# Regrouping the end of a state-space scan: weight sums by DMA, lag matrices later, two units split like the others

## The chip, the cores and the metric

The kernel runs on one core of one Trainium2 chip. The metric is the device time of one execution in microseconds. The engines are PE (matrix products), DVE (vector), ACT (scalar), POOL (GpSimd) and SP, which here only issues DMAs. ACT and POOL issue DMAs too. Each engine works through its own queue in order.

## The reference

One layer of a diffusion backbone over 1024 latent tokens with 256 context tokens, width 1024. The mixer is a two-directional diagonal state-space model; a SwiGLU block and a final norm follow.

```python
def s5_direction(u_ctx, u_lat, lam_re, lam_im, log_step, b_re, b_im, c_re, c_im):
    ...
    def run(u, h0):
        bu = jnp.einsum('lgh,gnh->lgn', u.astype(F32), b_bar)
        bu = bu.at[0].add(lam_bar * h0)
        a = jnp.broadcast_to(lam_bar, bu.shape)
        _, h = lax.associative_scan(_linear_combine, (a, bu), axis=0)
        return jnp.einsum('lgn,ghn->lgh', h, c_mat).real, h[-1]
    y_c, h_c = run(u_ctx, jnp.zeros(lam_bar.shape, lam_bar.dtype))
    y_l, _ = run(u_lat, h_c)
...
    def out(y, h):
        y = y.reshape(h.shape).astype(h.dtype) + d_skip * h
        g = jax.nn.gelu(y)
        return g * jax.nn.sigmoid(g @ w_glu + b_glu)
...
x = x + m_l[2][:, None] * y_l
h_l = modulate(rms_norm(x, norm_ffn[i]), m_l[3][:, None], m_l[4][:, None])
x = x + m_l[5][:, None] * swiglu(h_l, ffn_w1[i], ffn_w3[i], ffn_w2[i])
...
return rms_norm(x, norm_final)
```

There are 64 groups of 16 channels, each with 64 complex states per direction. Everything is float32.

## The kernel before, in words

**Tiling.** Tokens are cut into blocks of T = 8. Block states are scanned over 160 columns (32 of context, 128 of latent tokens), and inside a block the output is a Toeplitz product. The 64 groups form 4 quarters of 16, and each quarter two units of 8 groups: units 0 and 1 are quarter 0, units 6 and 7 quarter 3. A unit's mixer output is therefore the sum of a Toeplitz product of its inputs (`x_mm`, line 945, full height of 128 blocks) and of the products of the scanned states with the output weights `CL` (`states_mm`, line 922, one half of the 128 blocks; `states_all`, line 935, both halves). The backward direction needs its states in turned order: `turned` copies them.

**Scan.** `scan()` runs on DVE (line 77): 32 steps of two columns, then 63 of one. Each step has two products and two adds over all quarters. In its first, two-column part, the columns in between are left out; they are restored by quarter: quarters 0 and 2 by DVE in the gaps of the scan, quarters 1 and 3 by POOL, with `fill`, each call of which restores half the columns for all 16 elements.

**Work beside the scan.** `PROG1` is an order written out by hand for PE, ACT, POOL and SP, which run beside DVE's scan; `PROG2` is the order after it. Each token is a letter with an index:

- A: products of the modulation weights (line 531). B: turned input weights. M, m: modulation rows and columns.
- L, G: load of a quarter's output coefficients and sign change of part of them.
- C qp: part p (0 to 3) of quarter q of the output weights `CL`: two products on POOL, 128 x 1024 each, and their sum. `HOWS` says how the sum is made: E, an add on POOL (line 677); P, by PE through the identity, with two copies on ACT (lines 672, 673); Y, an accumulating DMA issued by POOL (line 675). `cts` names the temporary of the second product.
- F: restores left out columns on POOL.
- K: half of a quarter's lag matrices (`k_mats`, lines 809 to 817), copied out by ACT and written to DRAM from its queue (lines 821, 822). K needs all four parts of its quarter's `CL`.
- T u: loads a piece of a Toeplitz matrix from there (line 830, SP's queue), two pieces to a unit, into four places that are used in turn.
- R k: turned early half of unit k (on ACT). P k: Toeplitz and early states of unit k on PE, in two PSUM tiles. Y: copies of these to SBUF (line 993, ACT).
- After the scan: Z k, turned late half, on the engine that `ZEN` names (line 904 or 902); N k, late states of unit k; D k, their add to the early part on DVE; H k, GELU on ACT; I and J, transposes and their split for the GLU; W, V, w, l, x, g: GLU weights, gates and products.

In the kernel before, units 0 to 5 go this way: early part in `PROG1`, late states after the scan. Units 6 and 7 are left whole until after the scan: z copies all 128 turned columns, Q makes the Toeplitz product and all states at once, and GELU reads the two PSUM tiles.

**PSUM.** Tiles tagged `w` (`pw`) have three places that are used in turn: a new tile waits until the last reader of the tile in its place is through. K takes two accumulators, `kt` and `pm`; K6 takes two zeroed `pw` tiles.

Of the kernel before, what the change touches and what calls it, by code (L numbers as in the profile page):

```python
# [13 lines left out]
AF = mybir.ActivationFunctionType  # L14
# [3 lines left out]
P = 128  # L18
# [17 lines left out]
LN2H = 0.693359375
LN2L = -2.12194440e-4
# [5 lines left out]
def s5_ffn_kernel(tc, a, out):  # L43
# [3 lines left out]
    with ctx:  # L47
# [611 lines left out]
        def cl_ops(q, part, ct, how):  # L659
# [7 lines left out]
            def add():  # L667
# [8 lines left out]
                else:  # L676
# [232 lines left out]
        def yview(k, gp):  # L909
            return Y[:, k].rearrange("p t (a e h) -> p e a t h", e=2, h=HC)[:, gp]  # L910

        def states_mm(k, pts, half, hs, start):

            for a_ in range(4):
                for ri in range(2):
                    for d in range(2):
                        cs_ = slice(64 * (half ^ d), 64 * (half ^ d) + 64)
                        c0 = 31 + 64 * half
                        for gp in range(2):
                            ps = slice(64 * gp, 64 * gp + 64)  # L920
                            st = hs[ps, :, ri, a_] if d else STQ[k // 2][ps, c0:c0 + 64, ri, 8 * (k % 2) + a_]
                            PE.matmul(flat(pts[gp][cs_, a_]), st, flat(CL[k // 2][ps, ri, d, 4 * (k % 2) + a_]),
                                      start=start and ri == 0, stop=ri == 1 and (start or a_ == 3))

        def states_all(k, pts, hs):

            for a_ in range(4):
                for ri in range(2):
                    for d in range(2):
                        for c in range(2):  # L930
                            cs_ = slice(64 * c, 64 * c + 64)
                            for gp in range(2):
                                ps = slice(64 * gp, 64 * gp + 64)
                                st = hs[ps, cs_, ri, a_] if d else STQ[k // 2][ps, 31 + 64 * c:95 + 64 * c, ri, 8 * (k % 2) + a_]
                                PE.matmul(flat(pts[gp][cs_, a_]), st, flat(CL[k // 2][ps, ri, d, 4 * (k % 2) + a_]),
                                          start=False, stop=a_ + ri + d == 5)

        def x_mm(k, pool):

            pts = [pool([4, T, HC]) for _ in range(2)]  # L940
            for a_ in range(4):
                for gp in range(2):
                    g = 2 * a_ + gp
                    kq = KQ[(2 * k + g // 4) % 4][:, g % 4].rearrange("p (t h) -> p t h", t=T)[:, ::-1]
                    PE.matmul(pts[gp][:, a_], U[:, 8 * k + g, 32:160], kq, start=a_ == 0, stop=False)
# [3 lines left out]
        inner = {}
        HSe = [view(r, kb, [64, 2, 4]) for r, kb in ((RC[3], 14), (RC[3], 12), (RC[3], 14), (RC[3], 12), (RA, 2), (RA, 0))]  # L950
        HSl = [view(RA, STB * (i // 3) + 4.125 + 2 * (i % 3), [64, 2, 4]) for i in range(6)]
        HSq = {6: view(RA, 0, [P, 2, 4]), 7: view(RA, STB, [P, 2, 4])}

        def run(prog):


            for w in prog.split():
                op, i = w[0], int(w[1:])
                if op == "A":
                    ada(i)  # L960
                elif op == "M":
                    mod_cols(i)
                elif op == "K":
                    k_mats(*divmod(i, 2), [zeros(pw([15 * HC])) if i == 6 else kt, zeros(pw([15 * HC])) if i in (0, 1, 2, 3, 6) else pm[:, 0:15 * HC]])
                elif op == "L":
                    cs_load(i, S)
                elif op == "G":
# [4 lines left out]
                elif op == "C":  # L972
                    q, part = divmod(i, 10)
                    for f in cl_ops(q, part, cts[q][part], HOW[q][part]):
                        f()
                elif op == "F":
                    fill(*divmod(i, 10), *((RW, 0) if i >= 30 else (RC[3], 12)))
                elif op == "T":
                    toeplitz(i)
                elif op == "R":  # L980
                    turned(i, 0, HSe[i], S)
                elif op == "Z":
                    turned(i, 1, HSl[i], ENG[ZEN[i]])
                elif op == "z":
                    turned(i, 2, HSq[i], ENG[ZEN[i]])
                elif op == "P":
                    inner[i] = x_mm(i, pw)
                    states_mm(i, inner[i], 0, HSe[i], False)
                elif op == "Q":
                    inner[i] = x_mm(i, pe8)  # L990
                    states_all(i, inner[i], HSq[i])
                elif op == "Y":
                    S.copy(yview(i // 2, i % 2), inner[i // 2][i % 2])
# [774 lines left out]
```

## Time and profile before

| what | us |
|---|---|
| median of 3 runs (lowest, highest) | 1016.93 (1014.88, 1017.97) |
| profiled execution, its own time | 1015.21 |
| its span, first to last instruction | 1013.4 |
| PE busy | 959.4 |
| DVE busy | 780.4 |
| POOL busy | 763.4 |
| ACT busy | 438.9 |

The span is what the profile's rows add up to; the time of an execution is 1.8 us more. Busy times are sums over stages with different limits. The stage of the change lies between 129 us (the scan's first step) and about 260 us (the first GLU products). In the rows, `x4` behind an instruction is a count, a bracket holds the idle time before it and what ended that, and windows give busy times with counts, then the granted PE clock, the share of the DMA engines and GB/s.

### The profile page before, as it was taken

Reading aid. Unit: us, or ns where it says so; the run is one execution under the profiler, and the core shown is the slowest. Engines: PE = TensorE matmul, PEld = TensorE weight load, DVE = VectorE, ACT = ScalarE, POOL = GpSimd, SP = SyncE. Lnnn points to the kernel's source line nnn. Section 1 sums busy time; section 2 is a strip of 40 time slices with the busy share of each in tenths; the row PEclk is TensorE's granted clock in tenths of the full one; section 3 lists DMA queues with packets and bytes.
Section 4 is the critical chain, followed back from the end, with each engine's and each line's share of the span. In section 5 each row is a group of like instructions: output and inputs, shape, how many; then the busy total and the mean of one; then the engine's idle time right before and its main releaser. Section 6 shows DMA issues by size and latency. Waiting matters only on the chain. (4 is left out here: it accounts for less than half of the span.)

```text
span 1013.4 us, 18560 instructions
## 1 busy us (share of the span) xinstructions
PE 959.4 (95%) x6988; PEld 772.1 (76%) x6988; DVE 780.4 (77%) x1638; ACT 438.9 (43%) x860; POOL 763.4 (75%) x590
## 2 busy tenths in 40 slices
PE   5988798779999999999999999999999999999996
PEld 1466523679999988778888888888888888888885
DVE  7989699996356867877958677686959677686987
ACT  5478622335444663443343343324343343324337
POOL 5799998994672448979785878777786878777764
PEclk9999999999999999999999999999999999999998
DMA  9765997334512021011212111121212111121205
GB/s 336 280 135 95 280 346 247 95 84 138 188 46 80 2 104 63 27 44 46 73 42 83 42 52 42 50 66 53 73 42 83 43 52 43 46 70 53 73 22 166
DMA packets 48546, 98.96 MB, mean 98 GB/s; under 512 B 4284, under 2 KB 18876, under 8 KB 47176
## 3 DMA queue, kind: packets, MB, share of 16 engines
q1 hardware_dynamic: 43272, 86.64, 26.0%
q0 software_dynamic: 2016, 7.34, 3.9%
q10 hardware_dynamic: 3168, 3.79, 1.1%
q8 instruction: 55, 0.90, 0.4%
q14 instruction: 35, 0.29, 0.1%
HBM read 84.25 MB, written 6.17 MB: 89 GB/s over the span
## 5 line engine op out<-in xcount | busy, mean ns | idle before, releaser
L77 POOL TENSOR_TENSOR c<-rxc,c 128x512 fp32r<-128x512 f32 x128 | 166.6, 1315 | 53.5 <-ACT c L1222 52.7
L1282 PE MATMUL ut<-ra,c 128*128 128x512 f32 x400 | 155.7, 389 | 1.2 <-DVE ra L77 1.2
L1281 PE MATMUL ut<-ra,c 128*128 128x512 f32 x400 | 155.7, 389 | 0.2 <-ACT ra L1222 0.2
L1283 PE MATMUL ut<-ra,c 128*128 128x512 f32 x400 | 155.6, 389 | 0.0
L1222 ACT CAST c<-rxc 128x512 fp32r<-128x512 f32 x128 | 79.1, 622 | 147.0 <-PE xt L1576 53.3
L1576 PE MATMUL xt<-c,c 128*128 128x512 f32 x540 | 129.7, 389 | 0.0
L1576 PEld LDWEIGHTS xt<-c,c 128*128 128x128 f32 x540 | 101.4, 188 | 21.0
L77 DVE TENSOR_TENSOR ru<-ru,xt 128x1024 f32<-128x1024 f32 x90 | 107.3, 1215 | 10.9 <-PE xt L1576 7.9
L77 DVE TENSOR_TENSOR ru<-ut,ru 128x512 f32<-128x512 f32 x98 | 67.2, 686 | 43.0 <-PE ut L1283 37.6
L1282 PEld LDWEIGHTS ut<-ra,c 128*128 128x128 f32 x400 | 75.1, 188 | 17.0 <-POOL rxc L77 1.5
L1281 PEld LDWEIGHTS ut<-ra,c 128*128 128x128 f32 x400 | 75.1, 188 | 16.1 <-ACT ra L1222 0.6
L1283 PEld LDWEIGHTS ut<-ra,c 128*128 128x128 f32 x400 | 75.1, 188 | 15.5
L77 POOL TENSOR_TENSOR c<-rw,c 128x512 fp32r<-128x512 f32 (+1 forms) x29 | 41.1, 1417 | 37.8 <-ACT c L1222 37.8
L77 POOL TENSOR_TENSOR c<-ru,c 128x512 fp32r<-128x512 f32 (+1 forms) x39 | 57.1, 1465 | 10.1 <-ACT c L1222 5.7
L1281 PE MATMUL ut<-c,c 128*128 128x512 f32 x160 | 62.3, 390 | 0.8 <-DVE rxa L77 0.8
L77 POOL TENSOR_TENSOR rxc<-rxc 128x512 f32<-128x512 f32 x40 | 61.4, 1535 | 1.6
L1282 PE MATMUL ut<-c,c 128*128 128x512 f32 x160 | 62.2, 389 | 0.0
L1283 PE MATMUL ut<-c,c 128*128 128x512 f32 x160 | 62.2, 389 | 0.0
L1576 PE MATMUL ut<-c,c 128*128 128x512 f32 x216 | 51.9, 389 | 0.0
L584 PE MATMUL pv<-ru,c 128*64 128x160 f32 x512 | 45.0, 316 | 5.6 <-ACT rxa L388 1.8
L77 DVE TENSOR_TENSOR pe<-pe,ru 128x256 f32<-128x256 f32 x64 | 27.4, 429 | 29.5 <-ACT pe L1122 17.4
L77 DVE TENSOR_TENSOR ru<-ru,ut 128x512 f32<-128x512 f32 x76 | 47.3, 680 | 0.3
(444 smaller groups left out, 2569.1 us busy)
## 6 DMA issues: line engine op xcount, KB each, us to landing
c<-in_ada_w SPq DMA_DIRECT2D x46, 256.0 KB
rxc<-in_w SPq DMA_DIRECT2D x38, 256.0 KB
rxc<-in_w SPq DMA_DIRECT2D x19, 512.0 KB
ru<-in_w SPq DMA_DIRECT2D x11, 512.0 KB
rw<-in_w SPq DMA_DIRECT2D x11, 512.0 KB
ra<-in_ada_w SPq DMA_DIRECT2D x10, 512.0 KB
ra<-in_ada_w SPq DMA_DIRECT2D x18, 256.0 KB
ru<-in_xT SPq DMA_DIRECT2D x4, 1024.0 KB
```

What stands on the lines that cost most here:

```text
L77: eng.tensor_tensor(out=o, in0=x, in1=y, op=op)
L584: PE.matmul(pv[64 * (i % 2):64 * (i % 2) + 64, ri, c0:c0 + 160], w[:, i, 64 * ri:64 * ri + 64], U[:, 8 * b + 4 * j + i], start=True, stop= ...
L1222: S.copy(o[0], x)
L1281: PE.matmul(pu, wh, bh, start=start, stop=False)
L1282: PE.matmul(pu, wh, bl, start=False, stop=False)
L1283: PE.matmul(pu, wl, bh, start=False, stop=stop)
L1576: PE.matmul(pd, w[:, cs_], b, start=j in (1, 2, 4) and n == 0, stop=n == 2, skip_group_check=j not in (1, 2, 4))
```

## The change

- Five of the weight sums that POOL made are now accumulating DMAs (C21, C22, C30, C31, C32); the sum of C33 goes to PE. C23 stays on POOL. Before, C21 to C23 and C30 to C33 were all adds on POOL. A fifth temporary is added, in columns of quarter 1 that units 2 and 3 read early.
- Quarter 3 is restored by unit: `fill_k`, 8 elements at a time over all left out columns, in four POOL operations of 512 columns in place of eight of 256. F6 and F7 replace F30 and F31.
- Units 6 and 7 get early halves in `PROG1` (R6 P6 Y12 Y13, R7 P7 Y14 Y15), states only; unit 7's go to a scratch place. Their Toeplitz products come after the scan, in N6 and N7, in the same PSUM tiles as the late states; D6 and D7 add the parts. `states_all`, z and Q are gone.
- K4 goes behind P2 and next to K5, which gets two zeroed `pw` tiles (O5); O6 does the same ahead of K7 and K6, behind C33.
- Units 4 and 5: states first, then the Toeplitz product, in the same tiles.
- C33 goes from ahead of R5 to behind Y11.

```diff
-HOWS = "PPPP PPEE PEEE EEEE"
+HOWS = "PPPP PPEE PYYE YYYP"
-PROG1 = ("... T6 T7 C21 C22 C23 K4 R2 P2 Y4 Y5 K5 R3 P3 Y6 Y7 T8 T9 T10 T11 C30 C31 R4 P4 Y8 Y9 C32 C33 R5 P5 Y10 Y11 K7 K6 M2 m0 F30 F31")
-PROG2 = ("T12 T13 T14 T15 Z0 N0 Z1 Z2 D0 Z3 N1 D1 Z4 H0 H1 N2 D2 H2 w0 w1 l1 N3 Z5 D3 H3 N4 D4 z6 z7 I0 J0 I1 J1 H4 N5 D5 I2 J2 H5 I3 J3 W0 W1 x0 x1 x2 x3"
-         " Q6 H6 I4 J4 Q7 b0 I5 J5 H7 g03 g13 I6 J6 g23 g05 g15 I7 J7 V1 w20 w21 g26 x10 x11 x12 x13")
+PROG1 = ("... T6 T7 C21 C22 C23 R2 P2 Y4 Y5 O5 K4 K5 R3 P3 Y6 Y7 T8 T9 T10 T11 C30 C31 R4 P4 Y8 Y9 C32 R5 P5 Y10 Y11 C33 O6 K7 K6 M2 m0 F6 R6 P6 Y12 Y13 F7 R7 P7 Y14 Y15")
+PROG2 = ("T12 T13 T14 T15 Z0 N0 Z1 Z2 D0 Z3 N1 D1 Z4 H0 H1 N2 D2 H2 w0 w1 l1 Z6 N3 Z5 D3 H3 Z7 N4 D4 I0 J0 I1 J1 H4 N5 D5 I2 J2 H5 I3 J3 W0 W1 x0 x1 x2 x3"
+         " N6 D6 H6 I4 J4 N7 D7 b0 I5 J5 H7 g03 g13 I6 J6 g23 g05 g15 I7 J7 V1 w20 w21 g26 x10 x11 x12 x13")
...
-        cts = [..., [ct_[1], ct_[2], ct_[0], ct_[1]], [ct_[3], ct_[0]] * 2]
+        ct_ = [..., (RA, STB + 4.125)]
+        cts = [..., [ct_[1], ct_[3], ct_[0], ct_[2]], [ct_[3], ct_[0], ct_[4], ct_[3]]]
...
+        def fill_k(k):
+            tmps = [view(RA, 4.25 + 2 * i, [512]) for i in range(2)]
+            st, e = STQ[k // 2], 8 * (k % 2)
+            rot(st[:, 32:95:2, :, e:e + 8], st[:, 31:94:2, :, e:e + 8], LS[:, 0], 8 * k, E, tmps)
...
+        def ypart(k, gp):
+            return view(RA, 2 * STB + 4.25 + 2 * gp, [4, T, HC]) if k == 7 else yview(k, gp)
...
         def x_mm(k, pool):
-            pts = [pool([4, T, HC]) for _ in range(2)]
+            new = not isinstance(pool, list)
+            pts = [pool([4, T, HC]) for _ in range(2)] if new else pool
...
+                elif op == "O":
+                    KO[i] = [zeros(pw([15 * HC])) for _ in range(2)]
...
                 elif op == "P":
-                    inner[i] = x_mm(i, pw)
-                    states_mm(i, inner[i], 0, HSe[i], False)
+                    inner[i] = x_mm(i, pw) if i < 4 else [pw([4, T, HC]) for _ in range(2)]
+                    states_mm(i, inner[i], 0, HSe[i], i >= 4, i not in (4, 5))
+                    if i in (4, 5):
+                        x_mm(i, inner[i])
...
                 elif op == "N":
-                    late[i] = [pe8([4, T, HC]) for _ in range(2)]
-                    states_mm(i, late[i], 1, HSl[i], True)
+                    late[i] = [pe8([4, T, HC]) for _ in range(2)] if i < 6 else x_mm(i, pe8)
+                    states_mm(i, late[i], 1, HSl[i], i < 6)
                 elif op == "D":
-                        tt(yview(i, gp), po, yview(i, gp), ADD)
+                        tt(yview(i, gp), po, ypart(i, gp), ADD)
                 elif op == "H":
-                    if i in late:
-                        S.activation(Y[:, i], Y[:, i], AF.Gelu_apprx_tanh)
-                    else:
-                        for gp in range(2):
-                            S.activation(yview(i, gp), inner[i][gp], AF.Gelu_apprx_tanh)
+                    S.activation(Y[:, i], Y[:, i], AF.Gelu_apprx_tanh)
```

More of the change, by code (lines that the diff above doesn't have):

```diff
@@ L29 @@
 MAGIC = 12582912.0
-HOWS = "PPPP PPEE PEEE EEEE"
+HOWS = "PPPP PPEE PYYE YYYP"
 ZEN = "VVSVSVSV"
-PROG1 = ("A22 B0 A26 C02 G1 A30 A34 C03 A40 K0 A44 A48 C10 K1 L2 A54 G2 C11 A60 F10 C12 F11 C13 T0 T1 T2 T3 A64 M0 M1 K2 R0 P0 Y0 Y1 K3 L3 R1 C20 P1 Y2 Y3 T4 T5 G3 T6 T7 C21 C22 C23 K4 R2 P2 Y4 Y5 K5 R3 P3 Y6 Y7 T8 T9 T10 T11 C30 C31 R4 P4 Y8 Y9 C32 C33 R5 P5 Y10 Y11 K7 K6 M2 m0 F30 F31")
-PROG2 = ("T12 T13 T14 T15 Z0 N0 Z1 Z2 D0 Z3 N1 D1 Z4 H0 H1 N2 D2 H2 w0 w1 l1 N3 Z5 D3 H3 N4 D4 z6 z7 I0 J0 I1 J1 H4 N5 D5 I2 J2 H5 I3 J3 W0 W1 x0 x1 x2 x3"
-         " Q6 H6 I4 J4 Q7 b0 I5 J5 H7 g03 g13 I6 J6 g23 g05 g15 I7 J7 V1 w20 w21 g26 x10 x11 x12 x13")
+PROG1 = ("A22 B0 A26 C02 G1 A30 A34 C03 A40 K0 A44 A48 C10 K1 L2 A54 G2 C11 A60 F10 C12 F11 C13 T0 T1 T2 T3 A64 M0 M1 K2 R0 P0 Y0 Y1 K3 L3 R1 C20 P1 Y2 Y3 T4 T5 G3 T6 T7 C21 C22 C23 R2 P2 Y4 Y5 O5 K4 K5 R3 P3 Y6 Y7 T8 T9 T10 T11 C30 C31 R4 P4 Y8 Y9 C32 R5 P5 Y10 Y11 C33 O6 K7 K6 M2 m0 F6 R6 P6 Y12 Y13 F7 R7 P7 Y14 Y15")
+PROG2 = ("T12 T13 T14 T15 Z0 N0 Z1 Z2 D0 Z3 N1 D1 Z4 H0 H1 N2 D2 H2 w0 w1 l1 Z6 N3 Z5 D3 H3 Z7 N4 D4 I0 J0 I1 J1 H4 N5 D5 I2 J2 H5 I3 J3 W0 W1 x0 x1 x2 x3"
+         " N6 D6 H6 I4 J4 N7 D7 b0 I5 J5 H7 g03 g13 I6 J6 g23 g05 g15 I7 J7 V1 w20 w21 g26 x10 x11 x12 x13")
 LOG2E = 1.4426950408889634
@@ L693, in s5_ffn_kernel @@
                  14: [(3, range(4), 0, 8)]}
-        ct_ = [view(r, kb, [8, T, HC]) for r, kb in ((RW, 0), (RC[3], 0), (RC[3], 4), (RA, STB))]
-        cts = [[ct_[0], ct_[0], ct_[1], ct_[2]], [ct_[0], ct_[1], ct_[2], ct_[0]], [ct_[1], ct_[2], ct_[0], ct_[1]], [ct_[3], ct_[0]] * 2]
+        ct_ = [view(r, kb, [8, T, HC]) for r, kb in ((RW, 0), (RC[3], 0), (RC[3], 4), (RA, STB), (RA, STB + 4.125))]
+        cts = [[ct_[0], ct_[0], ct_[1], ct_[2]], [ct_[0], ct_[1], ct_[2], ct_[0]], [ct_[1], ct_[3], ct_[0], ct_[2]], [ct_[3], ct_[0], ct_[4], ct_[3]]]
         CL0 = cl_ops(0, 0, cts[0][0], SY) + cl_ops(0, 1, cts[0][1], SY)
@@ L864, in scan, with fill_q @@
                 one()
-        def fill(q, h, reg, kb):
-            tmps = [view(reg, kb + i, [256]) for i in range(2)]
+        def fill_q(q, h):
+            tmps = [view(RC[3], 12 + i, [256]) for i in range(2)]
             st, c0 = STQ[q], 32 * h
@@ L910, in yview, with states_mm @@
             return Y[:, k].rearrange("p t (a e h) -> p e a t h", e=2, h=HC)[:, gp]
-        def states_mm(k, pts, half, hs, start):
+        def ypart(k, gp):
+            return view(RA, 2 * STB + 4.25 + 2 * gp, [4, T, HC]) if k == 7 else yview(k, gp)
+        def states_mm(k, pts, half, hs, start, stop=True):
             for a_ in range(4):
@@ L922, in states_mm @@
                             PE.matmul(flat(pts[gp][cs_, a_]), st, flat(CL[k // 2][ps, ri, d, 4 * (k % 2) + a_]),
[L923 to L931, printed above, removed]
-                            for gp in range(2):
[L933 to L936, printed above, removed]
+                                      start=start and a_ + ri == 0, stop=stop and ri == 1 and a_ == 3)
         def x_mm(k, pool):
-            pts = [pool([4, T, HC]) for _ in range(2)]
+            new = not isinstance(pool, list)
+            pts = [pool([4, T, HC]) for _ in range(2)] if new else pool
             for a_ in range(4):
@@ L944, in x_mm @@
                     kq = KQ[(2 * k + g // 4) % 4][:, g % 4].rearrange("p (t h) -> p t h", t=T)[:, ::-1]
-                    PE.matmul(pts[gp][:, a_], U[:, 8 * k + g, 32:160], kq, start=a_ == 0, stop=False)
+                    PE.matmul(pts[gp][:, a_], U[:, 8 * k + g, 32:160], kq, start=new and a_ == 0, stop=not new and a_ == 3)
             return pts
         scan()
[L949 to L952, printed above, removed]
+        inner, KO = {}, {}
+        HSe = [view(r, kb, [64, 2, 4]) for r, kb in ((RC[3], 14), (RC[3], 12), (RC[3], 14), (RC[3], 12), (RA, 2), (RA, 0), (RA, 2), (RA, 0))]
+        HSl = [view(RA, STB * (i // 4) + 4 + 2 * (i % 4), [64, 2, 4]) for i in range(8)]
         def run(prog):
@@ L963, in run @@
                 elif op == "K":
-                    k_mats(*divmod(i, 2), [zeros(pw([15 * HC])) if i == 6 else kt, zeros(pw([15 * HC])) if i in (0, 1, 2, 3, 6) else pm[:, 0:15 * HC]])
+                    k_mats(*divmod(i, 2), KO.get(i) or [kt, zeros(pw([15 * HC])) if i < 4 else pm[:, 0:15 * HC]])
                 elif op == "L":
@@ L976, in run @@
                 elif op == "F":
-                    fill(*divmod(i, 10), *((RW, 0) if i >= 30 else (RC[3], 12)))
+                    if i < 10:
+                        fill_k(i)
+                    else:
+                        fill_q(*divmod(i, 10))
                 elif op == "T":
@@ L983, in run @@
                     turned(i, 1, HSl[i], ENG[ZEN[i]])
-                elif op == "z":
-                    turned(i, 2, HSq[i], ENG[ZEN[i]])
                 elif op == "P":
-                    inner[i] = x_mm(i, pw)
-                    states_mm(i, inner[i], 0, HSe[i], False)
-                elif op == "Q":
-                    inner[i] = x_mm(i, pe8)
-                    states_all(i, inner[i], HSq[i])
+                    inner[i] = x_mm(i, pw) if i < 4 else [pw([4, T, HC]) for _ in range(2)]
+                    states_mm(i, inner[i], 0, HSe[i], i >= 4, i not in (4, 5))
+                    if i in (4, 5):
+                        x_mm(i, inner[i])
                 elif op == "Y":
-                    S.copy(yview(i // 2, i % 2), inner[i // 2][i % 2])
+                    S.copy(ypart(i // 2, i % 2), inner[i // 2][i % 2])
                 elif op == "N":
-                    late[i] = [pe8([4, T, HC]) for _ in range(2)]
-                    states_mm(i, late[i], 1, HSl[i], True)
+                    late[i] = [pe8([4, T, HC]) for _ in range(2)] if i < 6 else x_mm(i, pe8)
+                    states_mm(i, late[i], 1, HSl[i], i < 6)
                 elif op == "D":
                     for gp, po in enumerate(late[i]):
-                        tt(yview(i, gp), po, yview(i, gp), ADD)
+                        tt(yview(i, gp), po, ypart(i, gp), ADD)
                 elif op == "H":
-                    if i in late:
-                        S.activation(Y[:, i], Y[:, i], AF.Gelu_apprx_tanh)
-                    else:
-                        for gp in range(2):
-                            S.activation(yview(i, gp), inner[i][gp], AF.Gelu_apprx_tanh)
+                    S.activation(Y[:, i], Y[:, i], AF.Gelu_apprx_tanh)
                 elif op == "I":
```

## The prediction

> **What bounds the kernel now.** I read the page's first part, then the windows of PE around the edit, then the timelines of DVE, PE, ACT, POOL and SP from 128 us to 260 us, and last the DMA queues.
>
> ```profile
> span 1013.4 us, 18560 instructions
> PE 959.4 (95%) x6988; PEld 772.1 (76%) x6988; DVE 780.4 (77%) x1638; ACT 438.9 (43%) x860; POOL 763.4 (75%) x590
> 230.62:245.27 14.65, 14.65 (x396) 1.00 0.72 210
> 245.27:258.44 13.17, 12.84 (x295) 1.00 0.41 121
> ```
>
> The 95% is an average over two regimes. From 230.62 us PE has next to no gap (14.65 of 14.65 us, then 12.84 of 13.17): what is taken from PE there comes off the end one for one, and what makes PE start later there is added one for one. Before it stands the scan, on DVE.
>
> ```profile
> 129.57 0.29 DVE L77 TENSOR_TENSOR ltb<-ra,lta 128x128 f32<-128x128 f32 x1
> 229.14 0.29 DVE L77 TENSOR_TENSOR ra<-ltc,ra 128x128 f32<-128x128 f32 x1
> L77 DVE TENSOR_TENSOR ltc<-ra,lta 128x128 f32<-128x128 f32 x95 | 27.7, 292 | 0.0
> 229.58 0.69 PE L922 MATMUL pe<-c,ra 64*64 64x128 f32 x4 [0.31 <-DVE ra L77]
> 230.62 0.64 PE L922 MATMUL pe<-c,ra 64*64 64x128 f32 x12 [0.35 <-DVE ra L904]
> ```
>
> 95 steps run from 129.57 to 229.43 us, 1.05 us each, without idle time (0.0 in the group). The edit leaves each of them alone, so I keep 229.4 as the scan's end. PE is ready there: its late states (N0) wait 0.31 us for the scan and 0.35 us for the turned copy on DVE. With 4 of N0's 64 pieces done early, its effective start is 230.5 us. PE's queue is in order: whatever the edit puts ahead of N0 must be done by 230.5, or the whole rest waits.
>
> **The change: what it takes from PE's bound part.**
>
> ```profile
> 247.65:251.95 4.30, 4.25 (x128) 4.05 (x128) 1.00 0.03 8
> 221.38:223.70 2.32, 2.28 (x64) 2.09 (x64) 1.00 0.67 208
> 252.32:254.20 1.88, 1.88 (x16) 1.76 (x16) 1.00 0.16 24
> 258.79 0.36 PE L1092 MATMUL pe<-c,c 128*128 128x256 f32 x1
> 232.91 1.29 DVE L77 TENSOR_TENSOR ru<-pe,ru 128x512 f32<-128x512 f32 x2 [1.47 <-PE pe L922]
> ```
>
> These are windows of line 935 (all states of a unit, 4.25 us), line 922 (half a unit's states, 2.28) line 945 (a unit's Toeplitz products, 1.88), PE's first GLU product and a DVE row. Q6 and Q7 fill 245.27 to 258.44 with some transposes: 4.25 + 1.88 each. N6 and N7 need 2.28 + 1.88. Saved: 2 x 1.97 = 3.9 us, plus the small gaps (0.33 us in the 13.17), which I count half: 4.1 us. New there are two adds of 1.29 us a pair for units 6 and 7 on DVE, and one GELU in place of two half ones. I cost them at nothing: the transposes that need unit 6 and 7 stand in PE's queue behind GLU products of units 0 to 3 and 0 to 5. Without that cover a pair would cost 1.3 us. The turned copies of the last quarter become half as long; they too are off PE's path.
>
> **What it puts ahead of N0.** All of units 6 and 7's early states (2 x 2.28), the PE sum of C33, and their ACT copies come into the queues before N0. I rebuild PE's queue from the end of P1, which the edit doesn't touch.
>
> ```profile
> 194.16 1.07 ACT L993 COPY ru<-pw 128x512 f32<-128x512 f32 x2 [3.63 <-PE pw L922]
> PE kt L809 <- POOL c L77: 3.1, 1, 3.1
> 223.59 0.27 PE L809 MATMUL kt<-c,rxa 64*16 64x112 f32 x1
> 185.40:189.15 3.75, 3.70 (x8) 1.44 (x8) 1.00 0.18 56
> 211.03 1.07 ACT L993 COPY ru<-pw 128x512 f32<-128x512 f32 x2 [2.33 <-PE pw L922]
> 211.99 0.63 ACT L902 COPY ra<-ra 128x512 f32<-128x512 f32 x1
> 225.33 0.36 ACT L821 COPY rw<-kt 128x240 f32<-128x240 f32 x1 [0.57 <-PE pm L817]
> 226.90 0.65 ACT L771 COPY pw<-r 128x240 f32<-128x240 f32 x2 [0.40 <-ACT rw L821]
> 229.37 0.36 ACT L821 COPY r<-pw 128x240 f32<-128x240 f32 x1 [1.82 <-issue]
> 230.88 1.14 ACT L902 COPY ra<-ra 128x512 f32<-128x512 f32 x2 [0.40 <-DVE ra L904]
> ```
>
> Prices: a lag matrix K 1.7 us (223.59 to 225.3), its evacuation on ACT 1.5 (229.37 to 230.88), two zeroed tiles 0.65, a PE sum 3.7 (the window of line 672), two Y copies and the turned copy R behind them 1.6 (211.0 to 212.6). PE's work alone from 194.1 to the end of P7 is 4 x 4.15 (P2 to P5) + 4 x 1.7 + 3.7 + 2 x 2.28 = 31.7 us, so without waits it would end at 225.8, well ahead of the scan. The waits decide.
>
> ```profile
> 174.34 7.97 POOL L77 TENSOR_TENSOR c<-rxc,rxa 128x1024 f32<-128x1024 f32 x4
> 195.20 2.35 POOL L77 TENSOR_TENSOR c<-c,c 128x1024 f32<-128x1024 f32 x1
> 220.95 2.38 POOL L77 TENSOR_TENSOR c<-c,rw 128x1024 f32<-128x1024 f32 x1
> 234.19 1.76 POOL L77 TENSOR_TENSOR ra<-ra,rw 128x256 f32<-128x256 f32 x2
> 130.77 0.88 POOL L675 DMA_DIRECT2D c<-rw  x1 [0.30 <-POOL rw L77]
> ```
>
> POOL first. A sum costs it 2.35; issuing it as a DMA 0.88 + 0.30 = 1.2. Five of these and the sum given to PE free 5 x 1.15 + 2.35 = 8.1 us. Its queue: C20 and C21 products to 182.3, C21 issued 183.5, C22 188.7, C23 (still on POOL) 195.1, C30 200.3, C31 205.5; C32's second product waits until P3 has read the columns its new temporary lies in (208.9 below), so C32 goes out at 212.1; C33's products 216.1. The two fills took from 223.3 to 235.95 with three small operations, about 6 each, so F6 is done near 222.6 and F7 near 228.5. Both are ahead of their readers below: POOL, which held K7 before (223.3 against 223.59), no longer holds anything.
>
> ```profile
> 189.87 0.60 SPq L830 DMA_DIRECT2D ra<-kd  x1
> 209.46 0.58 SPq L830 DMA_DIRECT2D ra<-kd  x1
> 232.30 1.27 SPq L830 DMA_DIRECT2D ra<-kd  x2
> 213.77 1.13 PE L945 MATMUL pw<-ra,ru 128*128 128x128 f32 x8 [2.77 <-DMA ra<-kd]
> 215.61 1.16 PE L945 MATMUL pw<-ra,ru 128*128 128x128 f32 x8 [0.71 <-DMA ra<-kd]
> q0 software_dynamic: 143, 0.52, 26.4%
> q0 software_dynamic: 122, 0.48, 81.0%
> q1 hardware_dynamic: 158, 0.29, 27.1%
> q1 hardware_dynamic: 301, 0.15, 59.5%
> ```
>
> Toeplitz loads: of four issued from 209.46 on, PE used the first at 213.77 and the second at 215.61, so 4.3 and 6.15 us after the issue; the issue comes 1.4 after ACT is through with the last lag matrix (230.88 to 232.30). T4 was issued at 189.87, so T5 is there at 196.0. P2, no longer behind K4 (whose 3.1 us wait for POOL goes), ends its states at 196.0 + 0.95 + 2.28 = 199.2 at best. New beside these loads is C22's DMA sum, issued about 188. One sum takes 26.4% of all engines over 10 us (118 to 128 us): 2.6 us. While it ran (124 to 127 us) it held 81.0% and the other queue 27.1%, where a Toeplitz load alone takes 59.5% (215 to 216 us): under half speed for 3 us, 1.6 us lost. Bounds 0 and 2.6; I take 1.6, P2's end 200.8.
>
> From P2's end, in us: K5's zeroed tiles at 1.75, K5 done 3.45, evacuated 5.0; P3's states, waiting for R3, done 7.9; T8 usable at 5.0 + 1.4 + 4.3 = 10.7, T9 at 12.6; Y6, Y7, R4 9.5, P4's states 11.8, its Toeplitz 13.7. P5 now begins with states, so R5, in ACT's queue behind Y8 and Y9, is exposed: 15.3, states 17.6, Toeplitz 19.5. PE sum of C33 23.2, its last copy (half of 1.07) 23.7, K7, begun during it, 25.1, K6 26.8. Then R6 stands on ACT behind K6's evacuation: 29.0, P6 31.3; R7 stands behind Y12 and Y13: 32.9, P7 35.2. So N0 starts at 200.8 + 35.2 = 236.0, 5.5 us late, with two gaps of 2.2 and 1.6 us on PE just before it. C31's sum goes out at 205.5, before T8's data moves; C32's hits T10 and T11, which have 2 us to spare: nothing.
>
> **Sum.** +5.5 - 4.1 = +1.4 us. The profiled execution took 1015.21 us (its span 1013.4 and 1.8 around it), 1.7 below the median of 1016.93; by the median 1018.3 us. With no loss to the DMA sums it is 1.4 - 1.6 = -0.2 (1016.7); with the full 2.6 there and once more on T8 and T9 +5.0.
>
> **Rivals.** (a) Slower by more than 0.3%: the DMA sums and the Toeplitz loads share the engines, and PE waits for a T. Price: 2.6 us per batch of loads that is hit, 1019.3 with one, 1021.9 with both batches; it decides when P2 ends after about 202.5 or T9 comes 2 us after P4's states. For it: the 81.0 against 27.1%. Against: C21 and C31 go out when little else moves.
> [...]
> (b) Faster: the waits on ACT and T shrink and P7 ends with the scan. Then N0 starts as before and 4.1 us are gained: 1012.8. For it: 31.7 us of PE work end at 225.8. Against: every wait counted is an in-order queue position that the diff writes down; three of the ten us would have to vanish.
> (c) PE's clock falls in the gaps before N0.
>
> ```profile
> 200.00:201.00 1.00, 1.00 (x7) 1.00 (x6) 1.00 (x7) 0.60 (x2) 1.00 (x1) 0.50 0.38 123
> 199.02 3.68 PE L945 MATMUL pw<-ra,ru 128*128 128x128 f32 x16
> ```
>
> After the 3.1 us wait for POOL the granted clock was 0.50 and Toeplitz took 3.68 in place of 1.88, 1.8 us lost; after the 2.77 us wait at 213.77 it did not fall. My gaps are 2.2 and 1.6, so I expect none; if it falls, 1020.1.
> [...]
>
> **How the numbers follow.** About 0.3% (3 us) is what a measurement of this kernel can tell from no change. My forecast, including its low bound and one batch partly hit, is within that: 0.57. Rival (a) at its price over 3 us 0.22, with (c) on top of a late chain 0.05: slower 0.27. Rival (b) and gains I don't see 0.16. The range leaves out the far ends of (a) and (b): 1013.2 to 1021.9; within the likeliest case 1016.5 to 1020.
>
> **What would show it.** Right: the scan ends near 229.4; PE has no idle 3 us before a lag matrix and no clock of 0.5 near 200; the first late states start near 236, behind two short PE waits for ACT's turned copies; PE is full from there, and the GLU begins about 1.4 us later than 258.8. Wrong: late states at 231 (b); PE waits of over 2 us for a load from the lag matrices' memory (a); POOL's fills ending after 230; PE idle again before the transposes of units 6 and 7, which would show the DVE adds uncovered.

## The result

The changed kernel takes 1034.01 us (median; 1032.80 to 1034.66) against 1016.72 for the kernel before, measured beside it: ratio 1.0166, 95% interval [1.0146, 1.0186]. In a later series with more runs it was 1.0119 [1.0097, 1.0141]. It is slower by 12 to 17 us, where a forecast of 1018.3 stood.

Rows of the page of the changed kernel, whose profiled execution took 1032.8 us:

```profile
span 1031.0 us, 18594 instructions
PE 969.3 (94%) x6996; PEld 778.2 (75%) x6996; DVE 779.8 (76%) x1642; ACT 443.6 (43%) x868; POOL 752.7 (73%) x581
q8 instruction: 55, 0.90, 0.4%
```

PE has the same number of products give or take eight (6996 for 6988), so the time went into waits and slow stretches. Its timeline from P1's end to the first GLU product; the bracket is the idle time ahead of a row and what ended it:

```profile
196.36 3.48 PE L942 MATMUL pw<-ra,ru 128*128 128x128 f32 x16 [3.20 <-DMA ra<-kd]
206.44 0.25 PE L809 MATMUL pw<-c,rxa 64*16 64x112 f32 x1 [1.68 <-issue]
217.61 1.16 PE L942 MATMUL pw<-ra,ru 128*128 128x128 f32 x8 [0.70 <-DMA ra<-kd]
220.27 2.08 PE L942 MATMUL pw<-ra,ru 128*128 128x128 f32 x8 [1.50 <-DMA ra<-kd]
228.90 1.02 PE L672 MATMUL pw<-c,r 128*128 128x512 f32 x2
236.75 0.50 PE L809 MATMUL pw<-c,rxa 64*16 64x112 f32 x22 [1.49 <-issue]
237.94 0.48 PE L931 MATMUL pw<-c,ra 64*64 64x128 f32 x2
240.26 3.68 PE L931 MATMUL pw<-c,ra 64*64 64x128 f32 x62 [1.29 <-ACT ra L908]
249.01 1.27 PE L931 MATMUL pe<-c,ra 64*64 64x128 f32 x32 [0.94 <-ACT ra L991]
256.03 2.37 PE L931 MATMUL pe<-c,ra 64*64 64x128 f32 x57 [2.28 <-issue]
276.32 0.36 PE L1086 MATMUL pe<-c,c 128*128 128x256 f32 x1
```

Read from the bottom: the GLU begins at 276.32, 17.5 us later than before (258.79), and 17.6 us is what the span grew by. N0, of which two products ran at 247.69, goes on at 249.01; before, four ran at 229.58 and it went on at 230.62. Ahead of it P6 begins at 237.94, when K6 is through, and K6 itself is 8.7 us late (229.27 before). So the loss has two places: PE's chain up to K6, and the block from K6 to the GLU, which grew from 29.5 to 38.3 us. P2's wait (3.20) and P4's two waits (0.70 and 1.50) for loads of Toeplitz matrices lie in the first place, and stalls marked "issue" in both.

DVE and POOL, each from its timeline:

```profile
251.31 1.29 DVE L77 TENSOR_TENSOR ru<-pe,ru 128x512 f32<-128x512 f32 x2 [19.73 <-PE pe L931]
213.09 2.03 POOL L77 TENSOR_TENSOR ra<-rxc,rxa 128x1024 f32<-128x1024 f32 x1 [5.64 <-PE pw L931]
215.41 0.86 POOL L675 DMA_DIRECT2D c<-ra  x1 [0.30 <-POOL ra L77]
220.81 2.47 POOL L77 TENSOR_TENSOR ra<-ra,r 128x512 f32<-128x512 f32 x2
228.26 2.85 POOL L77 TENSOR_TENSOR ra<-ra 128x512 f32<-128x512 f32 x2
```

DVE, which set N0's start before, now waits 19.73 us for N0. POOL waits 5.64 us for P3, because C32's second product overwrites columns that P3 reads; so C32's sum goes out only at 215.41, and the fills run from 220.8 to 231.1. PE's clock after three of the waits, around P4's waits and in the late stage (length, busy PE, PEld, DVE, ACT, POOL, then clock, share of the DMA engines, GB/s):

```profile
196.00:200.00 4.00, 3.64 (x22) 3.55 (x26) 4.00 (x24) 0.00 (x0) 3.70 (x4) 0.57 0.52 147
216.00:219.00 3.00, 2.07 (x35) 1.68 (x28) 2.79 (x13) 0.00 (x0) 3.00 (x3) 1.00 1.03 197
221.00:227.00 6.00, 5.68 (x71) 4.92 (x69) 5.62 (x24) 1.59 (x3) 5.92 (x5) 0.52 0.49 146
241.00:244.00 3.00, 2.94 (x54) 2.55 (x46) 0.00 (x0) 0.03 (x1) 0.00 (x0) 0.54 0.27 60
249.01:276.32 27.31, 25.03 (x566) 23.95 (x567) 14.72 (x25) 12.70 (x16) 5.58 (x3) 0.94 0.35 111
```

Three stretches ran near half clock. From 216 to 219 us, with P4's first wait and the start of its second, the DMA engines were full (1.03).

### The profile page after: what moved, and what is told of

The parts are those of the page before. It is cut to its first block, busy times and chain, and to the rows that moved or that the text cites. A ratio compares the mean times of both kernels' runs of the same rounds, so it can differ in the third digit from the quotient of the medians.

```text
span 1031.0 us, 18594 instructions
## 1 busy us (share of the span) xinstructions
PE 969.3 (94%) x6996; PEld 778.2 (75%) x6996; DVE 779.8 (76%) x1642; ACT 443.6 (43%) x868; POOL 752.7 (73%) x581
## 5 line engine op out<-in xcount | busy, mean ns | idle before, releaser
L1275 PEld LDWEIGHTS ut<-ra,c 128*128 128x128 f32 x400 | 75.1, 188 | 16.1 <-ACT ra L1216 0.6
L584 PE MATMUL pv<-ru,c 128*64 128x160 f32 x512 | 42.9, 308 | 7.5 <-POOL ru L77 2.8
L77 DVE TENSOR_TENSOR pe<-pe,ru 128x256 f32<-128x256 f32 x64 | 27.4, 428 | 29.5 <-ACT pe L1116 17.4
```

Source lines behind the costliest of these rows:

```text
L77: eng.tensor_tensor(out=o, in0=x, in1=y, op=op)
L584: PE.matmul(pv[64 * (i % 2):64 * (i % 2) + 64, ri, c0:c0 + 160], w[:, i, 64 * ri:64 * ri + 64], U[:, 8 * b + 4 * j + i], start=True, stop= ...
L1275: PE.matmul(pu, wh, bh, start=start, stop=False)
```

## The experiments

Four theories. **A**: the two lag matrices side by side outrun the supply of PE's instructions. **B**: the five sums by DMA hold back the Toeplitz loads. **C**: P6 and P7 stand ahead of N0 and hold the late stage. **D**: the half clock after the waits is the loss. Ratios are to the kernel before on the same chip, with 95% intervals; the changed kernel itself gave 1.0119 to 1.0166 from series to series, so differences under some 4 us between groups of runs are not read. The first four runs below were on one chip, on which the changed kernel took 1030.07 us in a later series (the square below).

**The sums back on POOL.** `HOWS` for the last two quarters; C33 stays on PE:

```diff
-HOWS = "PPPP PPEE PYYE YYYP"
+HOWS = "PPPP PPEE PEEE EEEP"
```

> The changed kernel with the five sums by DMA put back on POOL, the rest kept. Theory B: the waits for the Toeplitz loads at P2 (3.20 us) and at P4 (0.70 + 1.50) shrink, with the half clock after them, 4 to 6 us less than the changed kernel, 1028 to 1030, unless POOL's fills F6 and F7 (some 9 us later) then hold P6 and P7. Theories A and C: 1033 to 1035; with POOL's sums of 4 us each ahead of F6, C would even have it slower, up to 1038, since P6 and P7 stand ahead of N0.

1025.95 us, 1.0072 [1.0046, 1.0098]: 8 us less than the changed kernel's 1034.01, 4 less than its 1030.07 on the same chip. B's row by the second, past it by the first. Timelines of PE and POOL:

```profile
193.54 1.13 PE L942 MATMUL pw<-ra,ru 128*128 128x128 f32 x8 [1.01 <-DMA ra<-kd]
220.22 1.02 PE L672 MATMUL pw<-c,r 128*128 128x512 f32 x2
228.32 0.61 PE L809 MATMUL pw<-c,rxa 64*16 64x112 f32 x22 [1.76 <-issue]
229.72 0.69 PE L931 MATMUL pw<-c,ra 64*64 64x128 f32 x2
240.70 4.75 PE L931 MATMUL pe<-c,ra 64*64 64x128 f32 x145 [0.94 <-ACT ra L991]
266.25 0.36 PE L1086 MATMUL pe<-c,c 128*128 128x256 f32 x1
219.48 2.48 POOL L77 TENSOR_TENSOR ra<-ra,r 128x512 f32<-128x512 f32 x2
226.94 2.85 POOL L77 TENSOR_TENSOR ra<-ra 128x512 f32<-128x512 f32 x2
```

P2's wait for its load falls from 3.20 to 1.01 us, C33's sum on PE begins 8.7 us earlier (220.22 for 228.90), P6 8.2 earlier (229.72 for 237.94). And the fills begin at 219.48, earlier than with the sums by DMA (220.81): the DMA sums freed POOL for nothing, since POOL then waited for a PE that they had made late. From K6's end until N0 goes on there are still 10.9 us.

**Units six and seven whole again**, the rest of the change kept:

```diff
-... M2 m0 F6 R6 P6 Y12 Y13 F7 R7 P7 Y14 Y15
+... M2 m0 F30 F31
-... Z6 N3 Z5 D3 H3 Z7 N4 D4 ... N6 D6 ... N7 D7 ...
+... N3 Z5 D3 H3 N4 D4 z6 z7 ... Q6 ... Q7 ...
```

> The changed kernel with units six and seven whole after the scan, as in the kernel before (a fill of the last quarter at once, no early halves, both halves as one chain), the rest kept. Theory C (P6 and P7 take TensorE from 238.0 to 247.9 and two PSUM tiles of Y14 and Y15 hold N0 until 249.0): N0 starts at about 238 to 239, some 10 us earlier, the two units cost 1 to 4 us more in the late stage: 1025 to 1028. Theories A and B alone, if the scan's end and not the work ahead of N0 decided: 1033.

1023.80 us, 1.0072 [1.0048, 1.0095]: 1.2 us under C's row. From the end of K6 to the GLU:

```profile
234.73 1.55 PE L931 MATMUL pe<-c,ra 64*64 64x128 f32 x19
265.87 0.36 PE L1109 MATMUL pe<-c,c 128*128 128x256 f32 x1
```

N0 begins where K6 ends, and the block is 31.1 us in place of 38.3. (K6 too ended 3.2 us earlier here, at 234.8.)

**Lag matrices as before** (K4 ahead of P2, K5 behind it, K7's tiles as before):

```diff
-... C23 R2 P2 Y4 Y5 O5 K4 K5 R3 ... C33 O6 K7 K6
+... C23 K4 R2 P2 Y4 Y5 K5 R3 ... C33 K7 K6
```

> The changed kernel with the order of K4, K5, K7 and K6 and their PSUM tiles as in the kernel before, the rest of the change kept. Theory A (TensorE's instructions: two lag matrices side by side, 576 instructions, outrun the supply, 1.68 us of stall at K5 and 1.49 at K6): 3 to 4 us less than the changed kernel, about 1030. Theory B (the sums by DMA hold back the Toeplitz loads and so TensorE) and theory C (the early halves of units six and seven stand ahead of N0): no change, 1033 to 1035.

1030.36 us, 1.0117 [1.0079, 1.0154]: as A said against 1034.01, but no gain against the changed kernel's 1030.07 on the same chip. A is not borne out by the time; the stalls themselves are shown further down. The stall at K5 shrank from 1.68 to 0.30 us, and what was won was lost again: P4 waited 2.47 and 3.12 us for its two loads, K7 to K6 2.04 for zeroed tiles, and K6 ended at 237.3, 0.7 us earlier.

**Units four and five with Toeplitz first**, as before (`x_mm(i, pw) if i < 6`, states second):

> The changed kernel with units four and five in the order Toeplitz products, then states, as before; the rest kept. If the order states first loses time (TensorE meets the Toeplitz loads one stage later but at the half clock): 1032 or less. If it saves time, because the states fill TensorE's wait for the Toeplitz matrices: 1035 to 1037. Theories A, B and C expect little of it, 1033 to 1035.

1032.87 us, 1.0149 [1.0107, 1.0191]: the order makes no difference that shows.

**One part alone on the kernel before.** The five sums by DMA (`HOWS = "PPPP PPEE PYYE YYYE"`, the new scratch tiles):

> The kernel before with the five sums by DMA alone (C21, C22, C30, C31, C32, with their scratch tiles; C33 stays on POOL). Theory B: the loads of the lag matrices come late as in the changed kernel, K6 ends some 8 us later than 229.3 and the late stage with it: 1022 to 1026. Rival B' (the sums cost only together with the other edits, which need the matrices sooner): 1016 to 1019.

1019.06 us, 1.0027 [1.0010, 1.0044]: 2.7 us, not 8. A miss for B as I had put it. Waits of PE from 190 to 262 us (in total, times, longest):

```profile
PE pw L945 <- DMA ra<-kd: 4.4, 2, 4.1
PE kt L809 <- POOL c L77: 2.1, 1, 2.1
PE pe L922 <- issue: 0.4, 1, 0.4
```

In the old order K4 stands ahead of P2 and waits for POOL anyhow (2.1 us here, 3.1 before), and P2's loads arrive under that wait; only P4's wait is left, 4.4 us against 3.5. The split of units six and seven alone:

> The kernel before with units six and seven split alone (a fill and an early half of each ahead of N0, the late half after), the sums on POOL, lag matrices and units four and five as before. Theory C: N0 waits for P7 and starts some 10 to 12 us after K6's end, the late stage is 3 to 4 us shorter: 1023 to 1027. Rival C' (it was the late loads that held P6 and P7, so that without the sums by DMA they fit): 1015 to 1019.

1022.27 us, 1.0052 [1.0034, 1.0070]: 5.3 us, 0.7 us under C's row. N0 again begins 10.7 us behind K6's end (242.7 after 232.0). Both of these together:

> The kernel before with two parts of the change, the five sums by DMA (C33 on POOL) and units six and seven split; lag matrices and units four and five as before. Measured alone, the sums cost 2.7 us and the split 5.3. If the two parts add: 1024 to 1026. If the split turns every late load into time (K6's end no longer hides behind the scan's end): 1028 to 1031. Theory G (the lag matrices regrouped and C33's sum on TensorE take away the cover, so that the sums cost 7 to 8 us in the changed kernel): it stays at 1024 to 1026, and the rest of 1034 needs the regrouping.

1024.29 us, 1.0070 [1.0047, 1.0092]: 7.1 us, so they add as far as can be told. The rest of the 12 to 17 us needs the other parts.

**Both undone at once** (sums on POOL, units six and seven whole; C33 on PE):

> The changed kernel with the five sums on POOL and units six and seven whole; what is left of the change is the lag matrices side by side, C33's sum on TensorE, and units four and five with their states first. If B (8 us) and C (7 to 10 us) are the two causes and add up: 1016 to 1019, no difference from the kernel before. If theory A (the supply of TensorE's instructions, 1.4 to 1.8 us at each pair of lag matrices) costs beyond its place: 1020 to 1022.

1017.69 us, 1.0010 [0.9999, 1.0022]. With the five sums back on POOL and no split, no loss is left to measure. C33's sum is still on PE here and costs nothing that shows.

**Half of the sums.** C21 and C22 by DMA, C30 to C32 on POOL (`"PPPP PPEE PYYE EEEP"`):

> The changed kernel with only C21's and C22's sums by DMA; C30, C31 and C32 on POOL. Theory B, each sum held against the loads of its own moment: P2's wait of about 3 us for the loads T4 and T5 stays, P4's two waits shrink to those with all sums on POOL (0.7 us): 1028 to 1031. If the last three sums do all the harm: 1025 to 1027; if the first two: 1032 to 1034.

1029.70 us, 1.0128 [1.0101, 1.0156]: within what the changed kernel gave, so the time doesn't tell what half of the sums cost. The trace does show where: P2 waited 2.58 and 0.55 us for its loads, P4 not at all. The sums of C21 and C22 go with P2's wait alone.

**A square on one chip**, five rounds: the five sums by DMA or on POOL, and C33's sum on PE or on POOL, all else as in the changed kernel.

> The changed kernel itself (five sums by DMA, C33's sum on TensorE), beside the next three on one chip: a square of the two parts of the row of sums. All theories: 1029 to 1034, 1.2 to 1.7% over the kernel before.

> The changed kernel with the five sums on POOL, C33's sum on TensorE. Theory B: 5 to 8 us under f_dma_pe. If the difference of the first call was chance between calls: within 3 us of it.

> The changed kernel with C33's sum on POOL, the five others by DMA. C33's 3.6 us as a plain term of TensorE's chain: 3 to 4 us under f_dma_pe. Theory G (it uses up the slack that hid the late loads): 5 to 7 us under it. Hidden, because the late loads set the chain: within 2 us of it.

> The changed kernel with all six sums on POOL; what is left is the split of units six and seven, the lag matrices side by side, and units four and five with their states first. If the two parts add: f_pool_pe less 3 to 4 us, 1021 to 1023. Theory G, by which C33's sum costs only beside late loads: the same as f_pool_pe, since POOL then ends its fills 2.4 us later, 1024 to 1026.

| | C33 on PE | C33 on POOL |
|---|---|---|
| five sums by DMA | 1030.07, 1.0119 [1.0097, 1.0141] | 1027.72, 1.0092 [1.0063, 1.0121] |
| five sums on POOL | 1025.84, 1.0069 [1.0044, 1.0094] | 1020.47, 1.0025 [1.0011, 1.0039] |

The five sums cost 4.2 and 7.3 us by the columns, so they cost with and without C33's. C33's sum on PE costs 5.4 us beside sums on POOL, so G, that it costs only beside late loads, falls; beside the sums by DMA its 2.4 us are not told apart from nothing (the intervals overlap). All six sums together are 9.6 of the 12.1 us on this chip. C33 on POOL under DMA sums had been run once before:

> The changed kernel with C33's sum back on POOL (2.4 us there, behind C33's products and ahead of the fill F6), the four... other edits and the five sums by DMA kept. If the sum on TensorE is a plain term of the chain between P5 and K7 (3.6 us), and F6's 2.4 us of delay is hidden behind K7 and K6: 1030 to 1032. If the late loads and not the length of TensorE's chain set K6's end, or if P6 then waits for the later fill: 1033 to 1035. If it is what turns the 2.7 us of the sums by DMA into 7 (theory G): 1027 to 1029.

It gave 1028.25 us, 1.0119 [1.0093, 1.0144]. The time lay in G's row, but the ratio is that of the changed kernel in the square, and the square decides against G.

**P6 and P7 behind N3 and N4**, with the sums on POOL:

```diff
-... F6 R6 P6 Y12 Y13 F7 R7 P7 Y14 Y15
+... F6 R6 F7 R7
-... N3 Z5 D3 H3 Z7 N4 D4
+... N3 P6 Y12 Y13 Z5 D3 H3 Z7 N4 P7 Y14 Y15 D4
```

> The changed kernel with the five sums on POOL and with P6 and P7 moved from ahead of N0 to behind N3 and N4 (their fills and turned copies stay where they are). Theory C (P6 and P7 take 11 us of TensorE's time ahead of N0 for 4.6 us of products, the rest are waits for ACT and half clock): N0 starts when K6 ends, about 230, the late stage is 4.6 us longer than with P6 and P7 ahead: 1018 to 1021. Rival (the products themselves are what costs, wherever they stand): 1024 to 1026.

1023.17 us, 1.0061 [1.0040, 1.0082], not told apart from P6 and P7 ahead of N0 (1.0072). It lies between the two rows, nearer to the rival's: that the place costs is not shown. N0 did begin at K6's end, but the block to the GLU was 34.2 us, 2.3 shorter than with P6 and P7 ahead (36.5). Its largest group of waits is

```profile
PE pe L931 <- issue: 5.6, 3, 2.0
```

**The clock.** Idle products of the identity (`warm(n)` writes spare columns of `kt`'s bank) put into the waits:

```diff
-... C23 R2 P2 ... F6 R6 P6 ...
+... C23 R2 X22 P2 ... F6 R6 X8 P6 ...
 def x_mm(k, pool):
+    if k == 4: warm(4)      # and warm(9) ahead of the second half
```

> The changed kernel with idle products of the identity on TensorE in its waits: 22 ahead of P2's Toeplitz products, 4 and 9 in front of the two halves of P4's, 8 ahead of P6. Theory D (the clock falls to a half after these waits and costs 1.0 to 1.6 us each at P2, P5 and P6): clock near 1.0 at 196 to 200, 221 to 227 and 241 to 244, and 1029 to 1031. Without D, or if what comes next waits anyway: 1033 to 1035.

```profile
196.00:200.00 4.00, 4.00 (x43) 3.88 (x40) 4.00 (x24) 2.32 (x4) 3.52 (x2) 1.00 0.58 134
221.00:227.00 6.00, 6.00 (x95) 5.88 (x96) 5.59 (x24) 0.00 (x0) 5.62 (x8) 1.00 0.69 147
241.00:244.00 3.00, 1.95 (x63) 1.92 (x64) 0.00 (x0) 0.72 (x2) 0.00 (x0) 1.00 0.18 56
```

The clock is 1.00 in the three stretches, and the time 1034.38 us, 1.0167 [1.0144, 1.0190]: as the changed kernel. D is not borne out, but the test is not clean: at 210 to 218 us the clock was 0.57, where the changed kernel ran at 1.00 from 207 to 210 us, so part of the slow clock only moved. A second profile of the changed kernel itself, that of the square (1029.18 us), says more:

```profile
196.00:200.00 4.00, 3.41 (x54) 3.13 (x58) 4.00 (x24) 0.01 (x1) 3.70 (x4) 1.00 0.49 145
221.00:227.00 6.00, 5.19 (x78) 4.41 (x79) 5.62 (x24) 0.98 (x3) 5.92 (x6) 1.00 0.50 146
```

There the clock was 1.00 in two of the three stretches with no idle products, C33's sum began 2.8 us earlier (226.14), and the execution was 3.6 us shorter than the first one profiled. So the slow clock may be part of what one execution differs by from the next; a loss of 11 us is there with the clock at 1.00 in two of the three.

**The stalls marked "issue".** This run shows more than it was made for. Windows of PE from the end of a stall to the end of the lag matrix, first with the sums on POOL (K5, then K6), then with the idle products:

```profile
202.34:203.20 0.86, 0.86 (x82) 0.85 (x81) 0.80 (x4) 0.00 (x0) 0.86 (x1) 1.00 0.05 15
228.32:229.68 1.36, 1.36 (x108) 1.34 (x108) 0.35 (x1) 0.00 (x0) 1.36 (x1) 0.59 0.12 32
```

```profile
209.43:210.80 1.37, 1.37 (x126) 1.37 (x125) 1.27 (x6) 0.00 (x0) 0.00 (x0) 0.97 0.83 226
242.05:242.52 0.47, 0.47 (x50) 0.47 (x50) 0.00 (x0) 0.00 (x0) 0.00 (x0) 1.00 0.00 0
```

82 and 108 products are left behind the two stalls with the sums on POOL, and with Toeplitz first too. The 22 idle products, two records each, stand ahead of K4: 82 + 44 = 126. All 35 stand ahead of K7: 108 + 70 = 178, less 128 is 50. And with C33's eight products off PE, in the last kernel below, 100 are left in place of 108. In the changed kernel's first profile 128, 382 and 383 product records lie between its four stalls from 206.44 to 256.03 us: 1, 3 and 3 times 128, but for two records and one. So in these runs the stalls sit at fixed places of PE's instruction stream, 128 products with their weight loads or a multiple of that apart. I read them as waits for instructions; the page above counts 55 instruction transfers on q8 for 2 x 6996 instructions, 254 each. The stalls in the pairs of lag matrices took 1.4 to 3.6 us each.

The traces tell the transfers apart. For K6's stall and then N2's in the changed kernel: the stretch from the start of the 128 products ahead of it to the start of the transfer, and the transfer itself (234.29 to 235.44 us, 253.64 to 254.74), which holds one of the 16 engines (6.3%) all through:

```profile
233.50:234.29 0.79, 0.79 (x98) 0.79 (x78) 0.00 (x0) 0.17 (x1) 0.00 (x0) 1.00 0.00 0
q8 instruction: 1, 0.02, 6.3%
249.60:253.64 4.04, 4.04 (x137) 3.97 (x130) 1.90 (x4) 2.69 (x3) 0.00 (x0) 1.00 1.06 327
q8 instruction: 1, 0.02, 6.2%
```

PE went on 1.3 us behind each transfer; at the four stalls of this profile it was 1.29 to 1.50 us behind one. K6's 128 products were used up in 1.8 us, sooner than the 3.3 us from their start until the next could run. N2's took 4.2 us, but the next transfer began only after 4.0 us, with the DMA engines full (1.06), and PE went on 6.4 us after their start. A transfer begun after 0.8 us, as ahead of K6, would have been in time (an estimate from these rows: 0.8 + 1.1 + 1.3 us is under 4.2). So full engines go with a late transfer; that they cause it is not shown by a run of its own.

Whether data loads lengthen the stalls was to be seen from the GLU weights loaded later:

```diff
-... N2 D2 H2 w0 w1 l1 Z6 N3 ... Z7 N4 D4 I0
+... N2 D2 H2 Z6 N3 ... Z7 N4 D4 w0 w1 l1 I0
```

> The changed kernel with the three first loads of the GLU weights (2 MB) issued behind N4 and not ahead of N3. If these loads delay the pieces of TensorE's instructions and cause the stall of 2.28 us in N2 (theory A, in the form: the supply shares the DMA engines with the data): the stall falls to under 0.5 us, and the time to 1031 to 1033, unless the weights then come late for the first GLU product. If the stall comes from the rate at which N1 and N2 use up instructions: it stays at 2 us and the time at 1033 to 1037.

The edit moved nothing: SP's queue waits for no PE there and issued the weights at 246.07 us (245.36 in the changed kernel). Stall 1.82 us, time 1029.30, 1.0132 [1.0103, 1.0160]; it is one more run of the changed kernel, and what is known of the question is what the transfers above show.

**The version the runs point to**: only the lag matrices side by side, units four and five with states first, and C33 behind Y11; all sums on POOL, units six and seven whole.

> The version the runs point to: of the change only the lag matrices side by side and units four and five with their states first; all sums on POOL, units six and seven whole after the scan. K6 should end near 227 in place of 229.3, ahead of the scan's end. If the scan's end (229.4) then sets N0: the time of the kernel before, 1016 to 1018. If something of TensorE's earlier end reaches the end: 1013 to 1015.

1015.02 us against 1016.93, 0.9981 [0.9965, 0.9998]: about 2 us faster than the kernel before, with an interval that barely leaves out no change. Waits of PE:

```profile
PE pw L809 <- issue: 3.9, 2, 2.2
PE pe L931 <- DVE ra L77: 0.8, 1, 0.8
```

K6 ends at 227.0, N0 waits 0.8 us for the scan: in this kernel, as before, DVE decides.

## Why the prediction was wrong

The forecast's chain of PE beside the profiles (us from the span's start; "changed, second" is the square's profile of the same kernel):

| | forecast | changed | changed, second | sums on POOL |
|---|---|---|---|---|
| P2's states done | 200.8 | 202.0 | 201.1 | 198.2 |
| T8 used by P4 | 211.5 | 217.6 | 216.5 | 211.7 |
| C33's sum begins | 220.3 | 228.9 | 226.1 | 220.2 |
| K6 done | 227.6 | 238.0 | 235.3 | 229.8 |
| N0 goes on | 236.0 | 249.0 | 247.6 | 240.7 |
| GLU begins | 260.2 | 276.3 | 272.7 | 266.3 |

In the last column T8's use and C33's sum stand within 0.2 us of the forecast. That is luck in part: P2 was done 2.6 us earlier there, since the 1.6 us that the forecast counted for the sums by DMA are not in this kernel, and from there to C33's sum it took 22.0 us for 19.5, of which 1.40 are the stall in K5 that the forecast left out. The terms that failed can be told one by one; in the changed kernel's first profile the GLU's 16.1 us are 10.4 up to K6, 2.6 from there to N0, 3.1 behind it.

- **The price of the sums by DMA** was mis-sized: 1.6 us (bounds 0 and 2.6 a batch), measured 4.2 and 7.3 in the square. In the chains P6 began 8.2 us later than with the sums on POOL by the profiles above, 2.7 by the square's two. The step that failed is "C32's hits T10 and T11, which have 2 us to spare: nothing". With PE's chain late, C32 went out at 215.41 and not at 212.1, into T8's and T9's data (the full engines from 216 to 219 us: 41.3% for the sum's queue, 61.8% for the loads'), and P4 waited twice. But T8's load was itself issued 4.6 us late, at 211.82 for 207.2:

```profile
211.82 0.58 SPq L830 DMA_DIRECT2D ra<-kd  x1
```

Of P4's 6.1 us these 4.6 came from the chain ahead: 1.2 from P2, 1.9 from K4 and K5 with their stall, 1.5 from ACT's evacuation and the issue. The load's own delay was 1.5. Rival (a) named the mechanism at 22%; its 2.6 us a batch counted the load's delay and not the stages behind each other. The forecast did take P2 as bound by its loads once K4 was behind it; in the old order, where K4 covers them, the sums alone cost 2.7.
- **The supply of instructions** was not in the sum. K5 and K6 were put at 1.7 us each; their stalls of 1.68 and 1.49 us came on top, and one of 2.28 in N2.
- **P6 and P7** were put at 8.4 us from K6's end to N0. They took 8.1 in the kernel with sums by DMA and split alone, where the clock stayed at 1.00 from 237 to 240 us and the wait ahead of N0 was not there, and 10.4 to 12.5 in the others with the split ahead. The waits were those forecast, R6 and R7 behind ACT's evacuations; not in the sum of the changed kernel were 0.94 us for the copies Y14 and Y15 and the clock (P6's states 3.68 us for 2.28). The forecast had the gaps as too short for rival (c), a fall of the clock: it fell behind two waits of 1.49 and 1.29 us, with 2.2 us of products between.
- **The saving of 4.1 us** in the late stage was right in itself: with the sums on POOL N0 to GLU took 25.55 us for 28.3 (from the forecast's 230.5), of which 1.91 are a stall marked "issue", so 4.6 less in work. The changed kernel kept 1.0 of it (27.31): stall 2.28, clock 0.94.
- **The scan's end** near 229.4 was right. **POOL** no longer holding anything was right too, but worth nothing: 5.64 of its 8.1 us went into the wait for P3.
- **Rival (b)** was put too near: by the forecast's own times, N0 at 236.0 for 230.5, 5.5 of the ten us of waits had to vanish and not three. And the lag matrix's evacuation ends at 230.48, not at 230.88; the issue then comes 1.8 us behind it and not 1.4, so that sum stays.

By the ratios the changed kernel is 3 to 8 us worse than the parts measured alone add up to (2.7 + 5.3 + 1.0 us). Part of it is the lost cover of P2's loads, seen in the traces; how the rest divides is not settled.

## What to carry to other kernels

Work taken off an engine helps only if that engine was awaited (POOL's fills began at 220.81 us with five sums off it, at 219.48 with them on it): before moving a sum to a DMA, ask who waits for the loads that it will share engines with, and what covers that wait now. Work put ahead of an in-order bound stage can cost its chain of waits there, 11 us here for 4.6 us of products, and the saving behind it must be set against that; moving it behind won 2.3 us in one pair of profiles and nothing that shows in the time. The "issue" stalls of PE in dense runs of small products (1.49 us at K6, 2.28 in N2) were found by counting instructions and by the instruction queue's transfers, not by looking for a releaser.

## What the runs showed of the hardware

In the changed kernel's first profile PE stalled four times from 206.44 to 256.03 us, 128, 382 and 383 product records apart, and went on 1.29 to 1.50 us behind an instruction transfer. In the two pairs of lag matrices (stalls of 1.68 and 1.49 us) the 128 products before had been used up in 1.9 and 1.8 us, and the transfer began 1.0 and 0.8 us behind their start. At the stalls of 0.74 us (P3) and 2.28 us (N2) the 128 before lasted 4.5 and 4.2 us, and the transfer began 2.8 and 4.0 us behind their start, with the DMA engines full up to then (1.01 and 1.06). With the idle products, 44 or 70 instruction pairs more ahead, 126 products were left behind the stall for 82 (82 + 44), and 50 for 108 (108 + 70, less 128).

The share of the DMA engines by queue from 180 to 235 us in the changed kernel (packets, MB, share), where the accumulating sums are q0 and SP's plain loads q1:

```profile
q0 software_dynamic: 720, 2.62, 24.8%
q1 hardware_dynamic: 4304, 2.62, 17.8%
```

An accumulating transfer of 512 KB held the 16 engines for 24.8% of 55 us over five, 2.7 us, 1.4 times as long as the same bytes in SP's loads (17.8%), and landed 4.5 to 8.7 us after its issue.
